# A list scheduler gets a wider conflict rule and a seeded disturbance of its order of choice

## The chip, the cores and the metric

One core of one Trainium2 chip runs one program. The metric is the time of one execution on the device in microseconds (us), from the first to the last instruction and what lies around them; the value of a kernel is the median of its runs.

## What is computed

Two post-norm transformer layers over 512 latent tokens and 256 context tokens, width 1024, all in float32. Per layer:

```
mod  = silu(c) @ w_ada + b_ada                    (six vectors of 1024 for each of the two streams)
h    = x * (1 + scale1) + shift1
p    = h @ w_in                                   (1024 -> 2560: heads of groups A, B and C)
A: 6 heads, 2 key heads, window of 128 plus all context keys, one sink logit per head, 2-D rotary
B: 4 heads, difference of two softmaxes (width 32 each) over all keys, 2-D rotary, RMS norm
C: 6 heads, 8 x 16 neighbourhood with a bias per offset, plus all context keys
x    = layernorm(alpha * x + gate1 * (concat(A, B, C) @ w_o))
h    = x * (1 + scale2) + shift2
x    = layernorm(alpha * x + gate2 * ((silu(h @ w_gate) * (h @ w_up)) @ w_out))     (inner width 2816)
```

Context tokens go through the same weights in the first layer and read context keys only; in the second layer only their keys and values are needed. The output is the latent stream.

## The kernel before

**Tiles.** Activations stand transposed (channels on the 128 partitions, tokens along the free axis). Every large product is made of three matmuls per 128x128 block of weights, since both sides are split into a high part in the fast float32 format and a low remainder (`gemm_step`, lines 618 to 625). A weight chunk (128x1024) arrives by a DMA that SyncE issues, ScalarE writes its high half and GpSimd subtracts to get the low half (`halves`, lines 583 to 588); the subtraction reads two SBUF tensors. The projections are evacuated from PSUM by ScalarE and VectorE, rotated, and laid into per-head tiles in `proj` (lines 798 to 875). There the high part of each head is copied from one place in SBUF to another by `va.tensor_copy` (lines 859 and 870), which may go to VectorE or to ScalarE; in the profile these copies are the CAST instructions from R to R. `attend` (line 1025) takes one pair of heads: maxima of the scores (`maxima`, line 938), a transpose of them, a copy of them into a row of the query tile, then scores again with the maximum inside the product, Exp on ScalarE (`weights`, line 985) and the product with V. `attention` (line 1283) calls it 20 times in the first layer (three pairs of A, two of B with two halves each, three of C, for two streams) and 10 times in the second. `ln` (line 717) is the layer norm, `pair` and `ffn_out` the feed-forward part.

**Who sets the order.** Nothing is issued as it is written. Each call through an `Engine` object becomes an `Op` in `Program.ops` (`Program.add`, line 228), with the ops it must follow, an estimate of its duration for every engine that may run it (`duration`, line 418), and a rank for the kind of work it belongs to (`RANK`, line 173: on TensorE attention and layer norm work has rank 3, the modulation products 4, the large products 5; on ScalarE and VectorE attention, norm and weight splitting rank 4, the rest 3). `Program.schedule` (line 276) then runs a list schedule on the host: it walks through modelled time, and whenever an engine is free it takes, from the ops offered to that engine, the first in the order (rank, position in the program) whose inputs are ready and whose buffers are free. So a lower position wins among ops of one rank. The result is the order of instructions on each engine's queue, which engine runs an op that could go to two, and which buffer each tile gets. On the chip every engine then takes its queue strictly in order and waits where an operand is late.

**The conflict rule.** `Op.two` (set at line 271) marks an op with two inputs, `in0` and `in1`, both in SBUF. In the plan such an op isn't started on VectorE while another one runs on GpSimd, nor on GpSimd while one runs on VectorE if it could go elsewhere too (line 309); one that can only go to GpSimd is started and its duration lengthened by the rest of VectorE's (lines 333 to 336). An op with one SBUF input, such as the copies of lines 859 and 870, isn't marked.

**Filler.** After the schedule, `keep_busy` (line 365) looks for planned holes on TensorE of 0.23 us and more and puts a small matmul into each step of 0.23 us, where a PSUM bank is free (`IDLE0, IDLE1`, line 39). They are the matmuls of line 1408 in the profile; their results are read by nothing. All other instructions are issued at line 400 (memsets 398), so in the profile one goes by engine and tile rather than by line. The plan works with ops in the order of the program, some 400 ops to a thirty-second of it.

Of the kernel before, what the change touches and what calls it, by code (L numbers as in the profile page):

```python
# [36 lines left out]
COLD = 6.4  # L37

IDLE0, IDLE1 = 0.05, 0.23
DFF = 2816  # L40
KF = 22
NEG = -1e30
# [145 lines left out]
class Program:  # L188
# [39 lines left out]
    def add(self, alt, args, kw):  # L228
        o = Op()
        idx = len(self.ops)  # L230
        o.kw = dict(kw)
        if args:
            o.kw["ap"] = args[0]
            o.kw["constant"] = args[1]
        o.key = idx
        o.succ, o.slots = [], []
        pre = set()
        seen = set()
        for k, v in o.kw.items():
            if not isinstance(v, (View, bass.AP)):  # L240
                continue
            if isinstance(v, View) and id(v.slot) not in seen:
                seen.add(id(v.slot))
                o.slots.append(v.slot)
                v.slot.left += 1
            w = k in ("out", "accum_out", "ap")
            for c in self.cells(v):
                if c in self.writer:
                    pre.add(self.writer[c])
                if w:  # L250
                    pre.update(self.readers.get(c, ()))
        for k, v in o.kw.items():
            if not isinstance(v, (View, bass.AP)):
                continue
            w = k in ("out", "accum_out", "ap")
            for c in self.cells(v):
                if w:
                    self.writer[c] = idx
                    self.readers[c] = []
                else:  # L260
                    self.readers.setdefault(c, []).append(idx)
        if self.after is not None:
            pre.add(self.after)
        pre.discard(idx)
        o.wait = len(pre)
        for p in pre:
            self.ops[p].succ.append(idx)
        o.alt = {e: (call, duration(e, call.__name__, o.kw), RANK[e].get(self.kind, 3)) for e, call in alt}
        o.eng = alt[0][0]
        o.ready = 0.0  # L270
        o.two = all(k in o.kw and self.sbuf(o.kw[k]) for k in ("in0", "in1"))
        o.kind = self.kind
        o.start = None
        self.ops.append(o)

    def schedule(self):
        ops = self.ops
        free = {e: 0.0 for e in ENG}
        avail = {e: [] for e in ENG}

        def offer(i):
            for e, (_, _, r) in ops[i].alt.items():
                insort(avail[e], (r, i))
        for i, o in enumerate(ops):
            if o.wait == 0:
                offer(i)
        dma, table = 0.0, 0
        twice = {"dve": 0.0, "pool": 0.0}
        ev = [0.0]
        left = len(ops)  # L290
        t = 0.0
        while left:
            if not ev:
                raise RuntimeError("the schedule is stuck")
            t = heapq.heappop(ev)
            while ev and ev[0] <= t:
                heapq.heappop(ev)
            for e in ENG:
                if free[e] > t:
                    continue  # L300
                got = None
                if len(avail[e]) > 40:
                    avail[e] = [q for q in avail[e] if ops[q[1]].start is None]
                for j, (_, i) in enumerate(avail[e]):
                    o = ops[i]
                    if o.ready > t or o.start is not None:
                        continue

                    if o.two and (e == "dve" and twice["pool"] > t or e == "pool" and twice["dve"] > t and len(o.alt) > 1):
                        continue  # L310
                    places = []
                    ok = True
                    for s in o.slots:
                        if s.place is None:
                            pl = s.ring.find(s, t)
                            if pl is None:
                                ok = False
                                break
                            places.append((s, pl))
                    if ok:  # L320
                        got = j
                        break
                if got is None:
                    continue
                avail[e].pop(got)
                for s, pl in places:
                    s.ring.take(s, pl, t)
                o.start, o.eng = t, e
                o.call, o.dur = o.alt[e][:2]
                if e == "pe" and t < COLD:  # L330
                    o.dur *= 2

                if o.two and e in ("dve", "pool"):
                    x = "pool" if e == "dve" else "dve"
                    o.dur += max(twice[x] - t, 0.0)
                    twice[e] = t + o.dur
                left -= 1
                if e == "sp":
                    free[e] = t + 0.5
                    dma = max(dma, t + 1.1) + o.dur  # L340
                    o.end = dma + 0.8
                else:
                    if e == "act":
                        f = TABLE.get(o.kw.get("func"), table)
                        if f != table:
                            table = f
                            o.dur += 1.28
                    free[e] = o.end = t + o.dur
                heapq.heappush(ev, free[e])
                for s in o.slots:  # L350
                    s.left -= 1
                    s.t = max(s.t, o.end + 0.2)
                    if s.left == 0:
                        s.ring.release(s, s.t)
                        heapq.heappush(ev, s.t)
                for q in o.succ:
                    n = ops[q]
                    n.wait -= 1
                    n.ready = max(n.ready, o.end + SYNC[e].get(n.eng, 0.0))
                    if n.wait == 0:  # L360
                        offer(q)
                        heapq.heappush(ev, n.ready)
        self.end = max(o.end for o in ops)
# [54 lines left out]
def duration(eng, name, kw):  # L418

    out = kw["out"] if "out" in kw else kw["ap"]  # L420
    n = words(out)
    inp = next((kw[k] for k in ("in0", "in_", "rhs") if k in kw), out)
    a = inp.ap if isinstance(inp, View) else inp
    psum = a.space == bass.MemoryType.PSUM
    ptrs = sum(isinstance(kw.get(k), (View, bass.AP)) for k in ("scalar", "scalar1", "scalar2", "bias", "scale"))
    if eng == "pe":
        w = kw["lhsT"] if "lhsT" in kw else kw["in_"]
        w = w.ap if isinstance(w, View) else w
        rows, cols = w.ap[0][1], words(w)
        if name == "transpose":  # L430
            return 0.112
        if a.dtype == F32R:
            return max(n / 2400.0 * (1 if n >= 128 else 4) + 0.0135, 0.11)
        if a.dtype == BF16:
            return n / 2400.0 + 0.0135
        if cols < 128:
            return n * 4 / 2400.0 * cols / 128 + 0.005
        return 2 * max(n * 2 / 2400.0, 0.107) + 0.01
    if eng == "act":
        return 0.15 + n / 1200.0 + (0 if psum else 0.045) + (0.19 if "accum_out" in kw else 0.0) + 0.04 * ptrs  # L440
    if eng == "dve":
        if name == "reciprocal":
            return 0.07 + n / 160.0
        if name in ("tensor_scalar", "tensor_copy", "memset") and not psum:
            return 0.13 + n / 1920.0 + 0.06 * ptrs
        return 0.145 + words(inp) / 960.0 + 0.04 * ptrs + (0.08 if "accum_out" in kw else 0.0)
    if eng == "pool":
        if name == "tensor_tensor":
            return 0.25 + n / 464.0
        return 0.25 + n / 500.0 + 0.083 * max(0, ptrs - 1)  # L450
    return max(math.prod(q[1] for q in list((out.ap if isinstance(out, View) else out).ap)) * 4 / 360000.0, 0.05)
# [3 lines left out]
def hybrid_dit_kernel(ctx: ExitStack, tc, xc, small, cbc, w_ada, w_in, w_o, w_fi, w_fo, cbias, rope, consts, out):  # L455
# [32 lines left out]
    prog = Program()  # L488
# [20 lines left out]
    def T(cls="p", cap=None):  # L509
        return ring_t.new(cls, 1, cap)  # L510
# [714 lines left out]
    for k in range(KD):  # L1225
# [10 lines left out]
        x = xs[k]  # L1236
        for s, c0, nn in L0:
            A, B = modc(0, s, 1, k), modc(0, s, 0, k)
            hi, lo = h_nt(k, 0, c0, nn), h_nt(k, 1, c0, nn)
            t = T()[:, 0:nn]  # L1240
# [25 lines left out]
    for l in range(DEPTH):  # L1266
        lam_init = 0.8 - 0.6 * math.exp(-0.3 * l)
        e = []
        for q in range(2):
            d = S1("s")  # L1270
            tt = lamv[:, 256 + 32 * (2 * l + q):288 + 32 * (2 * l + q)]
            o = l * 128 + q * 64
            ve.tensor_tensor_reduce(out=tt, in0=lamv[:, o:o + 32], in1=lamv[:, o + 32:o + 64], scale=1.0, scalar=0.0,
                                    op0=ALU.mult, op1=ALU.add, accum_out=d)
            x = S1("m")
# [116 lines left out]
    n0, n = ROUNDS[1]  # L1392
# [9 lines left out]
    ffn_out(1, "fo", 8 * n0, range(6, 8), 0, n, [(256, 256)], [(0, 256, 256, sb_)])  # L1402
    ln(1, 1, 0, 256, 256, sb_, True)

    prog.schedule()
    prog.keep_busy(banks)
    with tc.manual_schedule():
# [113 lines left out]
```

## Time and profile before

| | |
|---|---|
| runs, median (lowest to highest) | 1905.76 us (1905.16 to 1906.55) |
| the profiled execution, its own time | 1907.67 us |
| its span, first to last instruction | 1905.9 us |
| mean granted TensorE clock, 1 is full speed | 0.990 |
| TensorE busy with matmuls | 1856.6 us |
| VectorE, ScalarE, GpSimd busy | 988.7, 758.1, 620.5 us |

Time is read in three ways: by engine (busy time), by stretch (busy time and granted clock of TensorE in slices of the span), and by single instructions in the order of time, with the idle time ahead of each and the engine whose result ended it. "PE" is TensorE, "PEld" its weight load, "DVE" VectorE, "ACT" ScalarE, "POOL" GpSimd. A busy TensorE may be busy with filler.

### The profile page before, as it was taken

How to read it: one execution, taken by the hardware profiler on the slowest of the kernel's cores; microseconds unless marked ns; L12 is line 12 of the kernel's file. 1: busy time of each engine (PE TensorE's matmuls, PEld its weight loads, DVE VectorE, ACT ScalarE, POOL GpSimd, SP SyncE). 2: the span in 40 equal slices, each digit the busy share in tenths (PEclk: the TensorE clock that was granted, in tenths of full speed). 3: DMA queues.
4: the chain of work that ended last, by engine and by line, in shares of the span. 5: the costliest groups of instructions: out<-in, count | busy, mean ns of one | idle time of the engine just before them, and what ended most of it. 6: DMA issues, size and time to landing. Idle time of an engine off the chain costs nothing.

```text
span 1905.9 us, 26437 instructions
## 1 busy us (share of the span) xinstructions
PE 1856.6 (97%) x10596; PEld 1556.8 (82%) x10596; DVE 988.7 (52%) x1607; ACT 758.1 (40%) x1365; POOL 620.5 (33%) x383
## 2 busy tenths in 40 slices
PE   9999999999999999999999999989999999999996
PEld 8877767788899888888888888766668998888886
DVE  3566645565577887322122695884554742202234
ACT  3456645556353211221122255444455552222232
POOL 0233411112254332233223362530123444444451
PEclk9999999999999999999999999999999999999998
DMA  8321212113224658321221221110114223233321
GB/s 309 97 67 56 86 53 78 41 55 119 89 78 134 188 190 294 113 67 56 67 67 58 65 100 33 42 61 12 34 39 130 82 67 99 92 97 100 100 67 45
DMA packets 52250, 172.72 MB, mean 91 GB/s; under 512 B 5920, under 2 KB 9376, under 8 KB 51744
## 3 DMA queue, kind: packets, MB, share of 16 engines
q1 hardware_dynamic: 52128, 171.04, 27.9%
q8 instruction: 83, 1.36, 0.3%
q14 instruction: 39, 0.32, 0.1%
HBM read 166.82 MB, written 4.19 MB: 90 GB/s over the span
## 4 chain that ended last, share of the span: by engine, by line
PE 88%; DVE 6%; ACT 2%; DMA 1%; issue 1%; POOL 1%; SPq 0%; POOLq 0%; ACTq 0%; DVEq 0%
PE PSB L400 85%; DVE R L400 3%; PE PSB L1408 3%; DVE TRB L400 2%; ACT R L400 1%; DMA WRB<-in_w_ada_dram 1%; ACT TRB L400 1%; DVE OZ L400 1%; DVE PSB L400 0%; DMA OZ<-in_w_ada_dram 0%; POOL OZ L400 0%; DMA WRB<-in_w_in_dram 0%; POOL TRB L400 0%; POOL R L400 0%; SPq L400 0%
## 5 line engine op out<-in xcount | busy, mean ns | idle before, releaser
L400 PE MATMUL PSB<-R 128*128 128x512 f32 (+5 forms) x8266 | 1572.4, 347 | 20.3 <-DVE R L400 10.9
L400 PEld LDWEIGHTS PSB<-R 128*128 128x128 f32 (+2 forms) x8266 | 1311.6, 190 | 226.6 <-issue 25.0
L400 POOL TENSOR_TENSOR R<-V,R 128x1024 fp32r<-128x1024 f32 x99 | 242.5, 2453 | 368.0 <-ACT R L400 362.0
L400 POOL TENSOR_TENSOR R<-WRB,R 128x1024 fp32r<-128x1024 f32 x74 | 180.9, 2446 | 265.3 <-ACT R L400 219.6
L400 ACT ACTIVATE TRB<-PSB 128x512 f32<-128x512 f32 (+2 forms) x337 | 163.1, 523 | 205.6 <-PE PSB L400 198.3
L400 ACT ACTIVATE R<-V 128x1024 fp32r<-128x1024 f32 x100 | 106.0, 1060 | 313.4 <-PE PSB L400 221.6
L400 PE MATMUL PSB<-TRB,V 128*128 128x512 f32 (+2 forms) x560 | 211.1, 509 | 1.0 <-DVE TRB L400 1.0
L400 DVE TENSOR_TENSOR TRB<-TRB,PSB 128x512 f32<-128x512 f32 (+1 forms) x69 | 39.9, 579 | 314.0 <-PE PSB L400 305.7
L400 DVE TENSOR_TENSOR R<-TRB,R 128x256 fp32r<-128x256 f32 (+3 forms) x150 | 168.4, 1130 | 45.8 <-ACT R L400 45.2
L400 PEld LDWEIGHTS PSB<-TRB,V 128*128 128x128 f32 x560 | 102.6, 194 | 69.1 <-issue 45.5
L400 ACT ACTIVATE R<-WRB 128x1024 fp32r<-128x1024 f32 x90 | 95.2, 1058 | 153.3 <-PE PSB L400 129.7
L400 DVE SCALAR_TENSOR_TENSOR OZ<-PSB,gp,OZ 128x512 f32<-128x512 f32 (+1 forms) x104 | 58.5, 584 | 183.1 <-PE PSB L400 183.1
L398 POOL MEMSET R<- 1x512 f32 (+1 forms) x64 | 26.1, 429 | 303.9 <-PE PSB L400 284.7
L400 ACT CAST R<-TRB 128x512 fp32r<-128x512 f32 (+3 forms) x133 | 72.7, 557 | 120.8 <-DVE TRB L400 119.8
L400 DVE CUSTOM_DVE_ANT_0 TRB<-V,RB,sm 128x1024 bf16<-128x1024 f32 x80 | 113.7, 1449 | 11.0 <-DMA V<-in_w_ada_dram 10.7
L400 DVE TENSOR_REDUCE TRB<-PSB 128x1 f32<-128x768 f32 (+1 forms) x92 | 69.3, 785 | 77.9 <-PE PSB L400 76.9
L400 DVE RECIPROCAL TRB<-TRB 128x512 f32<-128x512 f32 (+1 forms) x31 | 84.5, 2728 | 31.7 <-ACT TRB L400 30.4
L400 DVE TENSOR_TENSOR R<-PSB,R 64x256 fp32r<-64x256 f32 (+4 forms) x88 | 39.7, 456 | 86.0 <-ACT R L400 84.8
L400 ACT CAST R<-PSB 64x256 fp32r<-64x256 f32 (+6 forms) x115 | 46.7, 423 | 91.2 <-PE PSB L400 76.2
L400 POOL TENSOR_SCALAR OZ<-OZ,sm 128x256 f32<-128x256 f32 (+1 forms) x44 | 59.1, 1350 | 70.1 <-ACT R L400 58.5
L1408 PE MATMUL PSB<-mean_w 128*128 128x128 f32 x628 | 81.5, 277 | 0.0
L1408 PEld LDWEIGHTS PSB<-mean_w 128*128 128x128 f32 x628 | 76.6, 192 | 3.1 <-issue 1.8
(91 smaller groups left out, 1110.9 us busy)
## 6 DMA issues: line engine op xcount, KB each, us to landing
V<-in_w_fi_dram SPq DMA_DIRECT2D x66, 512.0 KB, 3.5
V<-in_w_ada_dram SPq DMA_DIRECT2D x56, 512.0 KB, 4.7
WRB<-in_w_in_dram SPq DMA_DIRECT2D x40, 512.0 KB, 3.6
V<-in_w_fo_dram SPq DMA_DIRECT2D x34, 512.0 KB, 3.5
WRB<-in_w_ada_dram SPq DMA_DIRECT2D x31, 512.0 KB, 3.5
WRB<-in_w_fi_dram SPq DMA_DIRECT2D x22, 512.0 KB, 3.6
WRB<-in_w_o_dram SPq DMA_DIRECT2D x16, 512.0 KB, 3.6
WRB<-in_w_fo_dram SPq DMA_DIRECT2D x12, 512.0 KB, 3.5
```

Of the source, the lines that this page charges most:

```text
L398: o.call(kw["ap"], kw["constant"])
L400: o.call(**kw)
L1408: prog.issue(lambda b: nc.tensor.matmul(out=PSB[:, 512 * b:512 * b + P], lhsT=mean_w, rhs=mean_w, start=True, stop=True))
```

## The change

The conflict rule is widened: an op with one SBUF input is marked too, on VectorE alone, unless it is a transpose on TensorE or a reciprocal. And the position in the program, by which ops of one rank are ordered, gets a random number between 0 and 12 added to it, from a seed for each of 32 equal stretches of the list of ops.

```diff
+SEEDS, WIDTH = (336512, 804259, 759321, 281271003, ... 878840, 253485), 12.0
...
-        o.two = all(k in o.kw and self.sbuf(o.kw[k]) for k in ("in0", "in1"))
+        ins = [o.kw[k] for k in ("in0", "in1", "in_") if k in o.kw]
+        o.two = ()
+        if ins and all(self.sbuf(x) for x in ins):
+            o.two = ("dve", "pool") if len(ins) > 1 else ("dve",) if alt[0][0] != "pe" and alt[0][1].__name__ != "reciprocal" else ()
...
+    def disturb(self, seeds, width):
+
+        n = -(-len(self.ops) // len(seeds))
+        for k, seed in enumerate(seeds):
+            part = self.ops[k * n:(k + 1) * n]
+            noise = np.random.default_rng(seed).uniform(0.0, width if seed else 0.0, len(part))
+            for i, o in enumerate(part):
+                o.key = k * n + i + noise[i]
...
-                insort(avail[e], (r, i))
+                insort(avail[e], (r, ops[i].key, i))
...
-                    if o.two and (e == "dve" and twice["pool"] > t or e == "pool" and twice["dve"] > t and len(o.alt) > 1):
+                    if e in o.two and (e == "dve" and twice["pool"] > t or e == "pool" and twice["dve"] > t and len(o.alt) > 1):
...
-                if o.two and e in ("dve", "pool"):
+                if e in o.two:
...
+    prog.disturb(SEEDS, WIDTH)
     prog.schedule()
     prog.keep_busy(banks)
```

The ops, their inputs and the arithmetic stay the same; the order on the queues, the engine of an op with a choice, the buffers and the filler come out of the new plan.

## Rows read from the trace of the kernel before

**Rows 1.** The page's first part, one line for all engines.
```profile
PE 1856.6 (97%) x10596; PEld 1556.8 (82%) x10596; DVE 988.7 (52%) x1607; ACT 758.1 (40%) x1365; POOL 620.5 (33%) x383
```

**Rows 2.** Stretches of 60 us: length, busy time of each engine, clock, DMA share, GB/s.
```profile
0.00:60.00 60.00, 57.23 (x567) 51.02 (x568) 23.38 (x65) 23.25 (x60) 9.58 (x26) 1.00 0.77 273
...
480.00:540.00 60.00, 60.00 (x342) 52.45 (x341) 33.32 (x48) 22.15 (x33) 17.01 (x9) 1.00 0.27 86
...
1860.00:1906.00 46.00, 30.27 (x206) 27.87 (x204) 23.49 (x64) 13.50 (x27) 7.44 (x6) 0.89 0.14 46
```

**Rows 3.** Filler in the costliest groups: busy us, mean ns, idle before.
```profile
L1408 PE MATMUL PSB<-mean_w 128*128 128x128 f32 x628 | 81.5, 277 | 0.0
```

**Rows 4.** Filler by stretches of 60 us: busy us of PE and PEld (count), clock.
```profile
0.00:60.00 60.00, 16.90 (x124) 14.91 (x124) 1.00 0.77 273
...
240.00:300.00 60.00, 10.21 (x78) 9.58 (x78) 1.00 0.17 53
300.00:360.00 60.00, 11.29 (x86) 10.38 (x86) 1.00 0.20 62
...
540.00:600.00 60.00, 6.67 (x54) 6.44 (x54) 1.00 0.28 89
...
1080.00:1140.00 60.00, 15.03 (x126) 14.98 (x126) 1.00 0.26 88
...
1260.00:1320.00 60.00, 4.71 (x32) 4.33 (x32) 1.00 0.12 36
1320.00:1380.00 60.00, 4.89 (x38) 4.71 (x38) 1.00 0.09 27
...
1860.00:1906.00 46.00, 2.33 (x18) 2.25 (x18) 0.89 0.14 46
```

**Rows 5.** PE in order of time, three instructions with the idle time ahead.
```profile
101.20 1.65 PE L400 MATMUL PSB<-R 65*128 65x512 f32 x4 [3.07 <-DVE R L400]
...
1206.55 2.65 PE L400 MATMUL PSB<-R 65*128 65x512 f32 x6 [3.29 <-DVE R L400]
...
1243.96 0.48 PE L400 MATMUL PSB<-ident,TRB 128*128 128x128 f32 x1 [4.68 <-DVE TRB L400]
```

**Rows 6.** All engines in order of time around 96 us.
```profile
93.73 0.42 DVE L400 CAST R<-R 64x512 fp32r<-64x512 f32 x1 [0.95 <-ACT R L400]
...
95.52 4.04 DVE L400 CAST R<-R 64x512 fp32r<-64x512 f32 x2 [0.60 <-ACT R L400]
95.56 1.52 POOL L400 TENSOR_TENSOR R<-TRB,R 64x512 fp32r<-64x512 f32 x1 [0.27 <-ACT R L400]
...
97.05 2.36 POOL L400 TENSOR_TENSOR R<-WRB,R 128x1024 fp32r<-128x1024 f32 x1
```

**Rows 7.** The same around 1235 us.
```profile
1233.54 5.68 DVE L400 CAST R<-R 32x512 fp32r<-32x512 f32 x4
...
1239.66 1.97 DVE L400 CAST R<-R 32x256 fp32r<-32x256 f32 x1
```

**Rows 8.** Stretches of 10 us, PE alone: length, busy, clock, DMA share, GB/s.
```profile
100.00:110.00 10.00, 8.80 (x22) 0.66 0.18 52
...
1200.00:1210.00 10.00, 6.71 (x24) 0.81 0.18 52
1210.00:1220.00 10.00, 10.00 (x35) 0.85 0.00 0
...
1240.00:1250.00 10.00, 6.04 (x20) 0.83 0.03 4
```

**Rows 9.** Copies of lines 859 and 870 on ACT, a group by form.
```profile
L400 ACT CAST R<-R 64x512 fp32r<-64x512 f32 x17 | 10.3, 619 | 0.2
```

**Rows 10.** All engines in order of time around 1406 us.
```profile
1404.36 2.37 POOL L400 TENSOR_TENSOR R<-WRB,R 128x1024 fp32r<-128x1024 f32 x1 [3.98 <-ACT R L400]
1404.85 2.42 DVE L400 CAST R<-R 64x256 fp32r<-64x256 f32 x2 [1.06 <-PE PSB L400]
...
1406.79 0.74 POOL L398 MEMSET R<- 1x256 f32 x2
```

More of the change, by code (lines that the diff above doesn't have):

```diff
@@ L39 @@
 IDLE0, IDLE1 = 0.05, 0.23
+SEEDS, WIDTH = (336512, 804259, 759321, 281271003, 944985004, 718318, 516341, 28779007, 132124, 227122, 977112010, 333935011, 951845012, 398475013, 444189014, 935110015, 262310, 551292017, 536926, 424140, 186056020, 745109, 157048, 219697, 622365, 244228, 350502, 143338027, 534949028, 535009029, 878840, 253485), 12.0
 DFF = 2816
@@ L302, in schedule @@
                 if len(avail[e]) > 40:
-                    avail[e] = [q for q in avail[e] if ops[q[1]].start is None]
-                for j, (_, i) in enumerate(avail[e]):
+                    avail[e] = [q for q in avail[e] if ops[q[2]].start is None]
+                for j, (_, _, i) in enumerate(avail[e]):
                     o = ops[i]
```

## The prediction

> **What bounds the kernel now.** First the line of all engines: TensorE is busy for 1856.6 of 1905.9 us, the next engine for 988.7 [rows 1]. Then the filler, since a busy TensorE may do nothing useful: 628 small matmuls take 81.5 us [rows 3]. So useful matmuls take 1856.6 - 81.5 = 1775.1 us, and 1905.9 - 1775.1 = 130.8 us are holes, filled (81.5) or open (49.3). The question for a change of order is where the holes lie. The table by stretches shows three kinds. The start (0 to 60) has 16.9 us of filler and 60 - 57.2 = 2.8 us open, under a DMA rate of 273 GB/s; the end (from 1860) has 2.3 us of filler and 46 - 30.3 = 15.7 us open, the last layer norm [rows 2, 4]. In the feed-forward parts TensorE is busy for 60.00 of 60 us without filler, of which one row stands for all [rows 2]: no order makes those shorter. What is left lies between: 81.5 - 16.9 - 2.3 = 62.3 us of filler and 49.3 - 2.8 - 15.7 = 30.8 us open, in the attention and around the layer norms.
>
> The single waits of TensorE show the open part. Three stand out: 3.07, 3.29 and 4.68 us, 11.0 together, all ended by VectorE [rows 5]. Just ahead of each, VectorE runs copies from SBUF to SBUF. A 64x512 copy takes 0.42 us alone, but two of them took 4.04 us at 95.5, while GpSimd ran two subtractions back to back; the copies' stretch ended at 99.56, the second subtraction at 97.05 + 2.36 = 99.41 [rows 6]. At 1233.5 four copies took 5.68 us and a later one 1.97 [rows 7]. And each of these stops is followed by a stretch at half clock: 1.2 in place of 2.4 GHz for a part of the next 10 to 20 us, shown as a mean of 0.66, 0.81, 0.85 and 0.83 [rows 8].
>
> **The change part by part.** The sum is made against the profiled execution's 1907.67 us (span 1905.9 and 1.8 around it), which lies 1.9 above the median of the runs, 1905.76. Less than 0.2% (3.8 us) can't be told from no change here. The choosing itself is done on the host and costs the chip nothing; no instruction is added or taken away but filler.
>
> *The wider rule.* It tells the plan what rows 6 and 7 show: a copy isn't begun on VectorE while a two-input subtraction runs on GpSimd. It goes to ScalarE (0.62 us there [rows 9]) or VectorE does something else first. What that is worth at the three stops: without the stall VectorE would be through 4.04 - 0.84 = 3.2 us earlier at the first, which covers its 3.07; at the second the profile shows the same pair of copies in 4.05 us; at the third 5.68 - 4 x 0.42 = 4.0 and 1.97 - 0.28 = 1.7 make 5.7 against 4.68. So up to 11.0 us open time. The clock adds: half clock for a share s of a stretch shows as a mean of 1 - s/2 and loses s/2 of the busy time in it, so (1 - 0.66) x 8.8 + 0.19 x 6.7 + 0.15 x 10 + 0.17 x 6.0 = 3.0 + 1.3 + 1.5 + 1.0 = 6.8 us. At most -17.8. At the other end nothing is gained, where the next late producer on VectorE, a rotation sum or a subtraction, holds the same matmul. I take two stops of three, -12: all three have one cause and the rule names it, but the plan around them is new. The copies that go to ScalarE cost nothing while it has room: 0.2 us more each, on an engine busy for 758 of 1906 us [rows 1]; if a copy stands ahead of an Exp that TensorE waits for, it costs 0.62 us once.
>
> One page bears on this. The row shows the copy ending 0.15 us behind GpSimd's instruction [rows 6], so it seems to have waited for the whole of it. The Trainium skill (SBUF — State Buffer, section "SBUF: two separate sides") says that VectorE and GpSimd share a pair of ports, which whoever starts first holds for its whole instruction, the other fully blocked; for a copy on both ports it names any GpSimd instruction, those without a second input too. The trace agrees for subtractions and not for memsets: of two copies begun at 1404.85 both ended by 1407.27, 0.54 us behind the subtraction's end at 1406.73, while two memsets ran from 1406.79 to 1407.53 [rows 10]. By the page, copies moved beside memsets would stall again; the sum goes by the row.
>
> *The disturbed order.* An op can now fall behind ops that stand up to 12 places later in the program, of its own rank and ready at that moment. A useful matmul takes 1775.1 / (10596 - 628) = 0.178 us on the mean [rows 1, 3], so on TensorE 12 places are up to 2.1 us. That is the size of the holes it could fill or tear. Within one accumulation the order is fixed by its PSUM bank; what changes is which bank, head or stream is served first, and with it the order on ScalarE and VectorE, the buffers and the moments of the loads. What can't be moved: start, end and feed-forward (above), and most of the filler around two layer norms, 6.7 and 15.0 us [rows 4], where everything waits for one chain of statistics. That leaves 62.3 - 21.7 = 40.6 us of filler in the attention, and 30.8 - 11.0 = 19.8 us open, 60 in all: the bound of the gain. The bound of the loss: 30 heads' pairs are worked through, each with a chain maxima, transpose, copy, scores; if in each the first matmul of a chain is late by half the width, 1.07 us, and nothing covers it, that is +32. I take the value by the nearest pair of rows, the same kind of work under two orders: the B heads' 120 us of the first layer carry 10.2 + 11.3 = 21.5 us of filler, the second layer's 4.7 + 4.9 = 9.6 [rows 4]. If the first falls to the level of the second that is -11.9; I take -12 for the whole.
>
> *The sum.* 1907.67 - 12 - 12 = 1883.7; less the 1.9 by which the profiled execution stands over the median, 1881.8, say **1882 us** (-1.3%).
>
> **The rivals.**
>
> *Torn chains (slower).* A plan is no better for being disturbed. TensorE takes its queue strictly in order; an op that heads a chain (the maxima of the next pair, or a transpose) and slips behind 6 to 12 ready matmuls of its rank makes VectorE and ScalarE start later, and the hole reappears where their result is due. Price 1.07 us per chain, up to 32. For it: the three ranks do not separate attention from attention, so the noise acts just there. Against it: the list schedule still starts only what is ready, and the holes are there to absorb slips. With the rule's -12 the point of decision is 11 of the 30 chains; with all 30 it is 1906 - 12 + 32 = 1926.
>
> *The stops only move (no change).* TensorE's stops are ended by VectorE, and the rule takes no work from VectorE but the copies that change engine. If the two-input ops beside GpSimd's subtractions become the next late ones, and the noise gives as much as it takes, the time stays at 1906, within 3.8.
>
> *All of it.* All three stops and their clock go (-17.8), and half of the 60 us of movable holes are filled (-30): 1858. For it: the filler sits in pieces smaller than 2.1 us between single maxima matmuls in the B heads, so other ready work could go there. Against it: where it sits TensorE often has nothing else that is ready, which is why the plan left the hole.
>
> *Copies beside memsets.* The page's rule taken at its word: each copy that the plan moves off a subtraction may meet a one-input GpSimd instruction. Two memsets took 0.74 us [rows 10]; if each of the 30 pairs lost one such 0.37 us on the path, the gain shrinks by 11 to 1893. Rows 10 speak against it; I give it 0.05.
>
> **How the numbers follow.** The forecast case, both terms in part, 0.50; all of it 0.17; beside memsets 0.05; no change 0.10; torn chains 0.18. Faster by over 0.2%: 0.50 + 0.17 + 0.05 = 0.72; within it 0.10; slower 0.18. The likeliest case alone reaches from 1907.67 - 1.9 - 17.8 - 20 = 1868 (the rule's whole gain and a third of the movable holes) to 1898 (8 us from the rule, nothing from the order). For eight in ten I extend it to 1860, near the case of all of it, and up to 1908, the whole case of no change; out lie most of the torn chains and a part of the best case.
>
> **What would show it.** Right: no VectorE copy from SBUF of 1 us or more beside a GpSimd subtraction, more of them on ScalarE; no stop of TensorE over 2 us between 60 and 1860; the four slices of rows 8 at 1.00; filler under 70 us, less of it in the first layer's B heads. Wrong on the rule: stops of 3 us still there, ended by a two-input VectorE instruction. Wrong on the order: filler as before or more, new stops ended by PE's own late chains, and feed-forward stretches that still show 60.00 of 60, so that any difference lies between 60 and 560 or between 1080 and 1560. The forecast falls if the median isn't under 1902.

## The result, and the profile after

The changed kernel takes 1831.77 us (1830.89 to 1833.02) beside 1905.46 us before (four runs; the 1905.76 above is the median of the first three): a ratio of 0.9613, 95% interval 0.9597 to 0.963, or 3.9% less. The forecast was 1882 with a range of 1860 to 1908. The direction was right and so were the places; the size was not.

The page's first part and its group of the filler, changed kernel:

```profile
PE 1805.2 (99%) x10326; PEld 1518.9 (83%) x10326; DVE 960.6 (53%) x1593; ACT 772.5 (42%) x1391; POOL 602.4 (33%) x369
...
L1425 PE MATMUL PSB<-mean_w 128*128 128x128 f32 x358 | 47.1, 277 | 0.0
```

The filler (line 1425 now) fell from 81.5 us [rows 3] to 47.1. With it the span of 1829.4 divides as before into useful matmuls, 1805.2 - 47.1 = 1758.1 us (1775.1 before), filler, and open holes, 1829.4 - 1805.2 = 24.2 us (49.3). So the 76.5 us of the span are 34.4 of filler, 25.1 of open holes, and 17.0 in useful matmuls, 9968 of them in both kernels. By an estimate the clock explains 11.1 us of the 17.0: over slices of 10 us, (1 - granted clock) x busy time, summed, is 11.5 us before and 0.4 after. Beside the four slices of rows 8 and the tail, these are the slices before with a clock under 1.00:

```profile
410.00:420.00 10.00, 9.57 (x56) 0.83 0.01 2
1400.00:1410.00 10.00, 7.26 (x31) 0.88 0.37 107
1410.00:1420.00 10.00, 10.00 (x52) 0.95 0.00 0
1430.00:1440.00 10.00, 9.03 (x54) 0.91 0.28 90
1440.00:1450.00 10.00, 10.00 (x54) 0.92 0.63 225
```

The other 5.9 us aren't explained by the clock and stay open. The subtraction gives filler all the time that it shares with useful matmuls; counted alone, the useful ones are busy for 1794.9 us before and 1770.8 after:

```profile
0.00:1905.90 1905.90, 1794.89 (x9968) 0.99 0.28 91
...
0.00:1829.40 1829.40, 1770.82 (x9968) 1.00 0.29 94
```

Where it went is seen by stages. They are cut at the statistics of the layer norms (the instruction that clamps the variance): start to the first norm, to the end of the first layer's feed-forward part, the second layer's attention, its feed-forward part (the tail of 24 us is left out). TensorE alone; columns are length, busy, granted clock, DMA share, GB/s. Before:

```profile
0.00:523.40 523.40, 508.35 (x3195) 0.99 0.29 96
523.40:1087.00 563.60, 563.60 (x3264) 1.00 0.36 116
1087.00:1499.38 412.38, 393.77 (x2113) 0.98 0.18 58
1499.38:1881.84 382.46, 382.46 (x1965) 1.00 0.26 82
```

The same stages of the changed kernel:

```profile
0.00:485.88 485.88, 481.44 (x3039) 1.00 0.31 103
485.88:1049.56 563.68, 563.49 (x3259) 1.00 0.36 116
1049.56:1422.62 373.06, 370.04 (x2015) 1.00 0.20 64
1422.62:1804.40 381.78, 381.78 (x1955) 1.00 0.26 82
```

The two attention stages lost 37.5 and 39.3 us, the feed-forward stages +0.1 and -0.7; the tail gained 0.9. The filler of the changed kernel in stretches of 60 us (busy time of PE and PEld, each with its count) answers to rows 4:

```profile
0.00:60.00 60.00, 11.19 (x80) 9.63 (x80) 1.00 0.77 278
60.00:120.00 60.00, 6.67 (x54) 6.55 (x54) 1.00 0.17 55
...
240.00:300.00 60.00, 0.00 (x0) 0.00 (x0) 1.00 0.24 72
...
1020.00:1080.00 60.00, 10.76 (x87) 10.90 (x88) 1.00 0.15 49
1080.00:1140.00 60.00, 2.68 (x22) 2.46 (x20) 1.00 0.23 75
...
1200.00:1260.00 60.00, 0.38 (x2) 0.38 (x2) 1.00 0.15 49
```

The filler of the start is still there (11.2 + 6.7 us, 16.9 before), and so is that around the second norm (10.8 + 2.7 for 15.0). In the B heads of the first layer it is gone, and in those of the second (now 1193 to 1299 us) 0.4 us is left.

The copies on VectorE, grouped by form, answer to rows 6 and 7; the longest wait of TensorE after the first 10 us answers to rows 5:

```profile
L416 DVE CAST R<-R 64x512 fp32r<-64x512 f32 x12 | 5.0, 419 | 3.3 <-ACT R L416 3.2
L416 DVE CAST R<-R 32x512 fp32r<-32x512 f32 x12 | 5.0, 417 | 2.8 <-ACT R L416 2.6
```

```profile
1082.43 1.13 PE L416 MATMUL PSB<-TRB,mean_w 128*128 128x256 f32 x4 [0.96 <-DVE TRB L416]
```

A copy alone takes 0.42 us (rows 6), and the means are 419 and 417 ns; the longest of all 33 copies on VectorE takes 0.48 us. So none is stalled. Past the start, where one load is waited for (2.24 us at 8.38), the longest wait of TensorE is 0.96 us where it was 4.68, and none of the 150 slices of 10 us up to 1500 shows a clock under 1.00.

What stands in the place of the filler is seen in the maxima of a pair of B heads for the 512 latent tokens, in the first layer. TensorE in order of time, and VectorE's reduction of one block, before:

```profile
254.94 0.59 PE L400 MATMUL PSB<-R 96*128 96x512 f32 x2
...
255.49 1.28 PE L1408 MATMUL PSB<-mean_w 128*128 128x128 f32 x10
255.57 0.96 DVE L400 TENSOR_REDUCE TRB<-PSB 128x1 f32<-128x768 f32 x1 [0.73 <-PE PSB L400]
...
256.58 0.62 PE L400 MATMUL PSB<-R 96*128 96x512 f32 x2
```

and such a pair in the changed kernel, TensorE alone:

```profile
296.51 1.27 PE L416 MATMUL PSB<-R 96*128 96x512 f32 x4
297.72 0.65 PE L416 MATMUL PSB<-WRB,cs 128*32 128x128 f32 x16
298.29 1.57 PE L416 MATMUL PSB<-R 128*128 128x512 f32 x6
```

Products of 96 rows that make 768 columns in two matmuls are the maxima of such a pair. Before, two of these matmuls come every 1.65 us: the next ones start 0.05 us after VectorE has reduced the last block (255.57 + 0.96 = 256.53), and filler bridges the time. After, two blocks are made at once and modulation products and other matmuls follow without a hole.

### The profile page after: what moved, and what is told of

It reads as the page before. It is cut to its first block, busy times and chain, and to the rows that moved or that the text cites. A ratio compares the mean times of both kernels' runs of the same rounds, so it can differ in the third digit from the quotient of the medians.

```text
span 1829.4 us, 25848 instructions
## 1 busy us (share of the span) xinstructions
PE 1805.2 (99%) x10326; PEld 1518.9 (83%) x10326; DVE 960.6 (53%) x1593; ACT 772.5 (42%) x1391; POOL 602.4 (33%) x369
## 4 chain that ended last, share of the span: by engine, by line
PE 95%; DVE 2%; ACT 1%; DMA 1%; POOL 0%; issue 0%; SPq 0%; POOLq 0%; ACTq 0%
PE PSB L416 93%; PE PSB L1425 1%; ACT R L416 1%; DVE OZ L416 1%; DVE R L416 1%; ACT TRB L416 0%; DVE TRB L416 0%; DMA OZ<-in_w_ada_dram 0%; POOL OZ L416 0%; DMA V<-in_w_fi_dram 0%; DMA WRB<-in_w_o_dram 0%; POOL R L416 0%; SPq L416 0%; POOLq L1533 0%; POOLq L416 0%
## 5 line engine op out<-in xcount | busy, mean ns | idle before, releaser
L416 PE MATMUL PSB<-R 128*128 128x256 f32 (+4 forms) x8266 | 1572.4, 347 | 3.2 <-DVE R L416 1.7
L416 DVE TENSOR_TENSOR R<-TRB,R 128x256 fp32r<-128x256 f32 (+3 forms) x165 | 175.1, 1070 | 47.4 <-ACT R L416 44.5
L416 DVE SCALAR_TENSOR_TENSOR OZ<-PSB,gp,OZ 128x256 f32<-128x256 f32 (+1 forms) x104 | 58.7, 584 | 189.0 <-PE PSB L416 188.8
L416 ACT ACTIVATE TRB<-OZ 128x256 f32<-128x256 f32 (+1 forms) x70 | 32.6, 476 | 101.2 <-DVE OZ L416 92.5
L416 DVE TENSOR_TENSOR OZ<-OZ,TRB 128x256 f32<-128x256 f32 (+1 forms) x138 | 73.9, 576 | 0.7
L416 ACT COPY TRB<-PSB 128x128 f32<-128x128 f32 (+4 forms) x122 | 48.3, 402 | 54.4 <-PE PSB L416 52.4
```

Of the source, the lines that this page charges most:

```text
L416: o.call(**kw)
```

## The experiments

All kernels below start from the changed one, so each diff is against it; `before` in the ratios is the kernel before, on the same chip as the run.

**The two halves of the change.** The rule alone (width 0):

```diff
-SEEDS, WIDTH = (336512, ... 253485), 12.0
+SEEDS, WIDTH = (336512, ... 253485), 0.0
```

> The wider conflict rule alone, the order of choice undisturbed. Theory S (the rule is worth the copies' stalls, a disturbed order is worth nothing by itself, and the rest is the choice of these very seeds): 1888 to 1896, no stop of TensorE over 2 us behind a copy, the copies on VectorE all near 0.42 us, filler as before or more (600 to 700). Theory D (any disturbance of the order spreads the work better): the same here. Theory R (the rule alone makes most of the gain, the order little): 1860 or less, filler near 360.

1885.43 us (before 1904.86), ratio 0.9903 (0.9885 to 0.9921). TensorE in the two attention stages, its filler, and the copies:

```profile
0.00:510.94 510.94, 496.81 (x3132) 0.99 0.29 98
...
1074.53:1476.90 402.37, 392.45 (x2153) 1.00 0.18 59
...
L1425 PE MATMUL PSB<-mean_w 128*128 128x128 f32 x604 | 79.0, 277 | 0.0
...
L416 DVE CAST R<-R 64x512 fp32r<-64x512 f32 x19 | 8.1, 426 | 0.6 <-ACT R L416 0.4
```

So the rule is worth 19.4 us. By the two profiled spans it is 22.5, 12.5 and 10.0 in the two attention stages (the profiled execution before was 2.8 us over the median beside this run). The filler hardly changes (81.5 to 79.0); open holes fall from 49.3 to 39.7, and the half clock, counted as above, from 11.5 to 4.4. Theory R falls. Theory S is near: no stop of TensorE over 2 us is left and the filler is as it said, but 1885 is 3 us below its range, and the rule doesn't end every stall of a copy: two 64x256 copies at 1384.18 took 2.41 us, one of them 2.0, beside a subtraction. The other half, the seeds with the old rule:

```diff
-        ins = [o.kw[k] for k in ("in0", "in1", "in_") if k in o.kw]
-        o.two = ()
...
+        o.two = ("dve", "pool") if all(k in o.kw and self.sbuf(o.kw[k]) for k in ("in0", "in1")) else ()
```

> The same seeds and width, the conflict rule of before. Theory S: the plan leaves the one that the seeds were fit to at the first copy, so part of the fit is lost, and the copies' stalls come back: 1865 to 1895, with copies of 1 us and more on VectorE and a clock under 0.997. Theory D: the disturbance helps as much and only the rule's worth is missing: 1845 to 1855. Theory R: 1900 or more.

1870.40 us, 0.9817 (0.9794 to 0.984), filler 64.0 us. The stalls of the copies are back:

```profile
L413 DVE CAST R<-R 32x512 fp32r<-32x512 f32 x16 | 14.1, 881 | 2.4 <-ACT R L413 2.0
```

The seeds gain 34.5 without the rule and 53.7 with it (1885.43 to 1831.77); the rule gains 19.4 without them and 38.6 with them. That is as theory S had it. By the two profiled spans the old rule costs 41.8 us: 16.9 of filler (64.0 for 47.1), which is fit that is lost, and the rest open holes and slower matmuls. How the last divides between the copies and other late operands wasn't measured.

**Is it the disturbance, or these seeds?** The same seeds, each moved to the neighbouring stretch:

```diff
-    prog.disturb(SEEDS, WIDTH)
+    prog.disturb(SEEDS[1:] + SEEDS[:1], WIDTH)
```

> The wider rule and the same 32 seeds, each given to the stretch ahead of its own (the first to the last): an order that is as much disturbed, by noise that was not meant for it. Theory S: within 12 us of the rule alone, 1880 to 1905. Theory D: 1825 to 1845, like the changed kernel. Theory R: like the rule alone, 1860 or less.

1883.66 us, 0.9889 (0.9874 to 0.9904), which is the rule alone within 2 us, and the filler is 80.8 us. And 32 other seeds (737687, 144003, ... 22618), the worst by its plan of some drawn at random:

> The wider rule, width 12, and 32 other seeds; of some drawn at random the ones whose plan has the most holes. Theory S (a disturbed order is worth what its plan is worth, and may as well lose): 1895 to 1912, slower than the rule alone by 10 or more, with more than 604 fillers. Theory D (any disturbance helps): under 1880.

1902.42 us, 0.9989 (0.9976 to 1.0002): slower than the rule alone by 17 and no different from before. The page's lines of the filler, first of the turned seeds and then of the other ones:

```profile
L1425 PE MATMUL PSB<-mean_w 128*128 128x128 f32 x620 | 80.8, 277 | 0.0
```

```profile
L1425 PE MATMUL PSB<-mean_w 128*128 128x128 f32 x680 | 87.5, 276 | 0.0
```

Theory D falls: of three disturbed orders of one width, one gains 54 us, one 2, one loses 17. The first is the change's own and the last was picked as a bad one, so they are no sample. They stand in the order of their filler (358, 620, 680 of them), a count of the planned holes in steps of 0.23 us. That this goes on was tried with nine seeds replaced so that the plan has fewer holes still:

> The changed kernel with 9 of its 32 seeds replaced, chosen because the plan with them has fewer holes. If the plan's order still decides on the chip: 1824 to 1830. If the plan has been fitted to its own errors by now: 1832 or more.

1826.34 us, 0.9584 (0.957 to 0.9599), 330 fillers: 5 us better than the changed kernel, and the best of all that ran. The count, which the plan gives before anything runs on the chip, goes with the time in all 13 kernels here that have the wider rule and filler, from 308 fillers to 680: a straight line through them, 1760 us and 0.21 us per filler, misses none by more than 6 us. The two with the old rule lie above it, the kernel before (628) by 15 us and the seeds with the old rule (482) by 10: in both, copies stall that the plan takes for free. Whether that is all of it wasn't measured.

**Does a stage keep its gain by itself?** The first nine seeds alone, up to the first norm:

```diff
-    prog.disturb(SEEDS, WIDTH)
+    prog.disturb(SEEDS[:9] + (0,) * 23, WIDTH)
```

> The wider rule, and the seeds of the first nine of 32 stretches alone (the first layer up to its first norm); the others undisturbed. If the two attention stages gain each from their own seeds: the first norm's statistics at 484 to 488 as in the changed kernel, the second layer's attention (norm to norm) 390 to 402 in place of 373, together 1852 to 1864. If the order of one stage works on in the next: the second layer's stage under 385, 1848 or less.

1861.24 us, 0.977 (0.9755 to 0.9785):

```profile
0.00:488.21 488.21, 483.12 (x3041) 1.00 0.31 102
...
1052.12:1454.78 402.66, 392.58 (x2153) 1.00 0.18 59
```

The first stage is as short as in the changed kernel to within 2.3 us, the second layer's attention as long as under the rule alone (402.4). The counterpart, the seeds from the 21st stretch on, `(0,) * 20 + SEEDS[20:]`:

> The wider rule, and the changed kernel's seeds from the 21st of 32 stretches on alone (from the second layer's attention); the first layer is undisturbed. If a stage's fit holds on its own, since the feed-forward part between makes the engines start anew: 1853 to 1860, the rule alone's 1885 less the 29 that the first nine seeds left over, second attention stage 371 to 378. If a fit holds only behind the very order that it was found with: second stage 385 to 402, 1868 to 1886.

1888.61 us, 0.9921 (0.9902 to 0.9939): nothing beyond the rule, and 3 us above the higher of the two ranges. The stage's line and that of the same with the 20th seed as well, `(0,) * 19 + SEEDS[19:]`, where the second layer's first projections lie:

```profile
1073.48:1476.12 402.64, 392.14 (x2149) 0.99 0.18 59
```

> As e10, with the seed of the 20th stretch as well, in which the second layer's first norms and projections lie; e10 had cut that stage's own beginning away. If a stage's fit holds on its own when it is whole: second attention stage 371 to 378, 1852 to 1862. If it holds only behind the first layer's order it was found with: second stage 385 or more, 1868 to 1886.

```profile
1074.74:1447.83 373.09, 370.23 (x2015) 1.00 0.20 64
```

1856.99 us, 0.9753 (0.9738 to 0.9767). The whole stage keeps its gain behind an undisturbed first layer: 373.09 us, beside 373.06 in the changed kernel. So the cut of the run before was wrong and not the idea: it had taken one stretch of the stage away, and with it all of its gain. The two stages add up, 24.2 + 28.4 = 52.6 of 53.7 us.

**How little does it take?** The first seed alone (the first loads, the modulation, the first projections):

```diff
-    prog.disturb(SEEDS, WIDTH)
+    prog.disturb(SEEDS[:1] + (0,) * 31, WIDTH)
```

> The wider rule and the first of the 32 seeds alone; it disturbs the start only (first loads, modulation, first projections, some 55 us). If the gain is many small fits spread evenly over the attention: 1880 to 1886, only the start shorter, by 5 at most. If a choice at the start decides how the stage behind it falls into place: first norm's statistics at 485 to 497 in place of 511, 1862 to 1872.

1866.32 us, 0.9804 (0.9787 to 0.982), 19 us under the rule alone, and the first norm's statistics come at 492.0. Filler by stretches (rule alone first, then with the first seed; the last stretch ends at the norm):

```profile
0.00:60.00 60.00, 16.90 (x124) 1.00 0.76 274
60.00:240.00 180.00, 0.00 (x0) 0.98 0.24 77
240.00:360.00 120.00, 13.57 (x100) 1.00 0.16 53
```

```profile
0.00:60.00 60.00, 11.19 (x80) 1.00 0.76 275
60.00:240.00 180.00, 7.77 (x60) 0.99 0.22 68
240.00:360.00 120.00, 0.00 (x0) 1.00 0.25 79
```

The start isn't shorter (16.9 us of filler, then 11.2 + 7.8); the 13.6 us in the B heads, some 200 to 300 us after the disturbed stretch, are gone. To see what in that seed does it, one load was moved in an undisturbed order, the first chunk of projection weights, from sixth on SyncE's queue to third, and in a second kernel to fifth (`-= 1.5`):

```diff
-    prog.disturb(SEEDS, WIDTH)
+    prog.ops[5].key -= 3.5
```

> The wider rule, no random numbers, and one op of the program moved: the load of the first chunk of projection weights, sixth on SyncE's queue, is chosen third. Theory K (the list schedule is so sensitive that one early tie decides how the attention behind it falls into place): like the first seed alone, first norm's statistics at 487 to 497, 1862 to 1872. Theory P (the gain of the first seed comes from its whole pattern): as the rule alone, 1880 to 1888.

> The same load moved by one place only, from sixth to fifth. Theory K, with no merit in an early load as such: this one falls elsewhere and gains little, 1878 to 1888. If the early load itself is what helps (its chunk is there sooner): a part of the gain, 1868 to 1877.

To third: 1868.22 us, 0.9816 (0.9799 to 0.9833). To fifth: 1885.01 us, 0.9899 (0.9885 to 0.9914). SyncE's queue under the rule alone, then with the load third:

```profile
1.18 0.90 SPq L416 DMA_DIRECT2D OZ<-in_w_ada_dram  x2
...
3.07 0.43 SPq L416 DMA_DIRECT2D WRB<-in_w_in_dram  x1
```

```profile
1.19 0.42 SPq L416 DMA_DIRECT2D OZ<-in_w_ada_dram  x1
1.66 0.42 SPq L416 DMA_DIRECT2D WRB<-in_w_in_dram  x1
```

One DMA issued 1.4 us earlier is worth 17.2 us, the same DMA moved by one place (0.5 us) is worth nothing. As with the first seed, the start isn't shorter, and the filler from 240 to 360 us is gone (0.00 for 13.57); the first norm's statistics come at 491.4. With the load fifth 13.47 us of that filler stay. Theory K holds in both forecasts: the plan far behind the load falls out in another way. Two points don't exclude that the load has to be early by more than one place, and which ops change places in between isn't known.

**Is there a rule behind the good order?** Instead of random numbers, maxima, transposes and the copy of a pair's maxima 40 places ahead:

```diff
+LEAD = 40
...
-        o.key = idx
+        o.key = idx - self.lead
...
         nmt = T("nm", 2)
+        prog.lead = LEAD
...
             va.tensor_copy(out=m, in_=bk[32 * hh:32 * hh + 1, 0:nq])
+        prog.lead = 0
...
-    prog.disturb(SEEDS, WIDTH)
```

> The wider rule, no random numbers; instead the maxima of every pair of heads, their transposes and the copy of them into the query tile get 40 places taken off their position, so that they are chosen ahead of the pair before. Theory H (what the chosen seeds chiefly do is to start the next pair's chain among the products of the present one): half or more of the seeds' 54 us, 1850 to 1862, and filler well under the 604 of the rule alone, in the attention above all. Rival F (the gain is the sum of many small fits, that no rule of this kind gives): 1875 or more, filler 550 or more.

1865.76 us, 0.9793 (0.9777 to 0.9809), 65.0 us of filler in 502 pieces:

```profile
0.00:494.09 494.09, 485.14 (x3041) 0.99 0.30 101
...
1057.69:1457.50 399.81, 389.99 (x2141) 1.00 0.19 60
```

Between the two theories: 19.7 of the 54 us. In the first layer it gives 16.9 of the 25.1 us that the change's order takes off the stage; in the second 2.6 of 29.3. That the early chain is the cause in the first layer isn't shown: one load moved by three places takes 19.5 us off the same stage (510.9 to 491.4) and clears the same filler. In the second layer it is at most a small part. Why the good orders fit better, op by op, stays open. With seeds of its own on top, found without those of the change:

> Maxima early as in e5, and on top of it seeds of its own, chosen with none of the changed kernel's to start from, so that the plan has few holes. Theory S (any order with as few holes gives the same, no seed is special): 1820 to 1832, faster than the changed kernel or level with it. Rival (the changed kernel's own seeds are special on the chip, beyond the plan): 1838 or more.

1828.68 us, 0.9606 (0.9588 to 0.9623), 308 fillers. Level with the changed kernel, with other seeds throughout and the maxima early: the changed kernel's seeds aren't special.

**What is the filler worth in the good order?**

```diff
-    prog.keep_busy(banks)
+    prog.idle = []
```

> The changed kernel's order without its 358 filler matmuls; leaves out no part of the result. If the holes that are left are too short and too few for the clock to fall: 1830 to 1836, clock 0.99. If the clock still hangs on them: 1840 to 1870, slices of 10 us under 0.9 in the attention and around the norms.

1839.30 us, 0.9653 (0.9638 to 0.9667), clock 0.985: 7.5 us slower, just short of what the second case gave. The clock falls at the start, around the second norm and from 1390 to 1430 us, where filler stood, but not at the first norm (1.00 from 480 to 540 us, where 5.9 us of filler are gone); slices of 30 us at the start and around the second norm, without filler:

```profile
0.00:30.00 30.00, 19.47 (x202) 0.75 0.93 353
...
60.00:90.00 30.00, 25.96 (x135) 0.89 0.14 52
...
1060.00:1090.00 30.00, 20.83 (x113) 0.83 0.26 92
```

## Why the prediction was right and wrong

**The places were right.** Start, tail, feed-forward parts and the filler around the norms were called immovable, and stayed (above): 16.9 us of filler at the start became 17.9, 6.7 and 15.0 around the norms 6.3 and 13.4. Every sign that the prediction named came: no copy of 1 us on VectorE; 91 of them on ScalarE, where 57 were (28 + 20 + 21 + 22 for 17 + 6 + 18 + 16, by form); no stop over 2 us; clock 1.00 in the four slices; filler under 70; feed-forward stretches unchanged.

**The rule's term was a little small:** -12 taken, -17.8 as its bound, -19.4 measured alone. "Two stops of three" is the step that failed: all three went. The argument for two, that the plan around them is new, has something in it (the rule alone has a new stop of 1.98 us, ended by ScalarE), and the 19.4 us are what is left after it.

**The order's term was mis-sized:** -12 taken, -53.7 measured, near its bound of -60. The step that failed is "the value by the nearest pair of rows", that the first layer's B heads fall to the level of the second's. Two things are wrong in it. It lets one stage move and holds the other still, while both fell to almost no filler (0 and 0.4 us). And it treats the disturbance as one thing with a typical effect; there is none: the same width gave -54, -2 and +17 us by the seeds. What the order is worth is decided by the one plan that these seeds make, and the changed kernel's plan has 358 fillers where the rule alone has 604. That the seeds were picked for it isn't shown; the turned and the other seeds make it likely. As long as that plan isn't known, the effect is open between the two bounds, from -60 to +32, and the three measured values lie inside. The bounds of both terms together, 1905.8 - 17.8 - 60 = 1828, are 4 us from the result. The range stopped at 1860 and so gave up its own lower bound.

**The accounting by kind.** By the profiled spans, the rule's 22.5 us are 9.6 of open holes, 2.5 of filler and 10.4 of useful matmuls, 7.1 of these by the clock; the prediction had 11.0 and 6.8 for all three stops. The order's 54.0 us are 15.4, 31.9 and 6.6, 4.0 of these by the clock. Of the 40.6 us of filler called movable, 33.5 went in all. The prediction priced the clock only behind the three long stops; 4.6 us more hung on shorter ones (1.86 us at 410 and 1.83 at 1407 before, and several under 0.6 ahead of 1440), and belong to any term that closes holes. Its holes of 130.8 us are too large by the time that filler shares with useful matmuls: 1905.9 - 1794.9 = 111.0.

**The rivals.** "Torn chains" named the size of what another draw did (17 us slower than the rule alone, 1902 and not 1926), with more filler; that chains were torn there isn't shown. "All of it" named what happened and priced half the holes, 1858. "Stops only move" was wrong under the rule. "Copies beside memsets" asked for stalls of the copies, and in the changed kernel there are none.

## What to carry to other kernels

Where a host program picks the order by a greedy rule, the order is a lottery ticket, and a small edit can be one too: 17 us came from one load moved by three places. Judge a change of such a kernel by several draws, and choose among draws by the holes of a plan whose conflicts match the chip; the rule that made this plan truer was worth twice as much with the order that goes with it (38.6 for 19.4 us), part of it fit that is lost without the rule. And when a term has known bounds and no mechanism that picks a value between them, the range goes to the bounds.

## What was not expected of the hardware

A copy from SBUF to SBUF on VectorE can wait for two GpSimd instructions in a row. In the seeds with the old rule one 64x256 copy took 3.24 us, from 127.64 to 130.88 us (such copies take 0.31 on the mean in the changed kernel), over the rest of one subtraction that ended at 128.37 and all of the next, 128.34 to 130.73. Two orders without a common seed, of 308 and 358 fillers, come out 3 us apart. Filler that takes 47 us of TensorE's time saves 7.5 us: without it, some stretches where it stood show 0.75 to 0.89 of the full clock, and others stay at 1.00.
